# Two weight sums of the feed-forward tiles: adding DMAs in place of GpSimd additions

## The chip, the cores and the metric

The kernel runs on one core of one Trainium2 chip. The metric is the device time of one execution in microseconds; the number for the kernel before is the median of three runs. One further execution was profiled, and every view below comes from its trace.

## The reference, cut to what matters

The program computes two transformer blocks on a sequence of 512 tokens of width 1024, in 32-bit floats. Both end with a gated feed-forward network, and only these two networks are touched:

```
f = (silu(h @ w_gate) * (h @ w_up)) @ w_down          # first block
x = x + (silu(h @ w_ffn_gate) * (h @ w_ffn_up)) @ w_ffn_down   # second block
```

The hidden width is 2816, which is 22 tiles of 128 columns. Norms, attention and the other projections stand before, between and behind the two networks and are the same in both kernels.

## The kernel before, in words

**Arithmetic.** A 32-bit matrix is held as two parts, a high part (`hi`, a copy by ACT into the format that the matmul reads) and the rest (`lo`, a subtraction by DVE); a product takes three matmuls (hi·hi, hi·lo, lo·hi). So each weight tile that comes from HBM as `raw` is split by ACT and then DVE into `wt` or `u`.

**The products of one tile.** The feed-forward networks use a scheme of Strassen's kind. For tile f the gate and up products are formed from seven products of sums of weight blocks with sums of blocks of h. G is the gate's weight tile and U the up weight tile, each 128x1024 with a low half (columns 0 to 511) and a high half. `Tile.sums` (L390) forms four sums in place, in this order: G.lo += U.lo (L397), U.lo += U.hi (L398), U.hi = G.lo + U.hi (L399), G.hi = U.hi + G.hi (L400). All four run on GpSimd (POOL), 128x512 each. The third and fourth overwrite U.hi, so the split of the original U.hi (`w22`, DVE's u<-raw,u) has to be done before.

**Opening tiles ("head").** `first` and `second` are the two products with the unchanged gate weights. For the first 12 tiles of FFN 1 and the first 8 of FFN 2 (`t.head`) they are computed in an opening, before the main loop, from a load of the gate weights of their own; the other tiles do them in the main loop, and need the split of the unchanged G there.

**The main loop** (`ffn`, L414 on) runs over f from 0 to 21. An iteration does, among others: `finish(f-1)` on DVE, whose first operation t<-f,u reads PSUM; `left_g(f-1)`, whose lo halves are DVE's t<-t,t and u<-t,u with both inputs in SBUF; the products with s2 and s3; the splits of the next tile's U and G (`wb`, `wa`; DVE's wt<-raw,wt); the loads of tile f+3 and of a down weight; `blocks` of tile f+2 (the split of U.hi and, for a tile without an opening product, of G); the product with p1; `sums` of tile f+2; the down product of f-1; the products with a22 and p4. Between the products DVE reads PSUM banks (t<-u,tp, t<-f,t) that the next product goes on accumulating into.

**What sets the order.** `behind` fixes the order on PE, ACT and DVE in the main loop to the order of the code. POOL and the load queue (SP) are left to the scheduler. On POOL it puts the first two additions of the next tile behind the last two of this one, so in time they run as soon as that tile's loads have landed. All loads are issued by SP, 512 KB each; six raw buffers go round, three to an iteration, and a load waits until DVE and ACT have split what its buffer held.

Of the kernel before, what the change touches and what calls it, by code (L numbers as in the profile page):

```python
# [13 lines left out]
ALU = mybir.AluOpType  # L14
# [20 lines left out]
def transformer_pair(ctx: ExitStack, tc: tile.TileContext, A: dict, out: bass.AP, spill: dict):  # L35
# [6 lines left out]
    nc = tc.nc  # L42
# [340 lines left out]
    class Tile:  # L383
# [8 lines left out]
        def sums(self):  # L392

            lo, hi = slice(0, 512), slice(512, 1024)
            G, U = self.G, self.U
            add = nc.gpsimd.tensor_tensor
            add(G[:, lo], G[:, lo], U[:, lo], op=ALU.add)  # L397
            add(U[:, lo], U[:, lo], U[:, hi], op=ALU.add)  # L398
            add(U[:, hi], G[:, lo], U[:, hi], op=ALU.add)  # L399
            add(G[:, hi], U[:, hi], G[:, hi], op=ALU.add)  # L400

# [867 lines left out]
    U, Y, G = u_fill, pool_fill, gate_fill  # L1269
# [317 lines left out]
```

## Time and profile before

| | |
|---|---|
| Median of three runs | 1355.0 us (1354.44 to 1356.34) |
| Profiled execution, its own time | 1355.67 us |
| Its span, first to last instruction | 1354.0 us |
| Granted TensorE clock, mean | 0.992 of full speed |
| PE busy | 1298.9 us, 96% |
| DVE busy | 983.5 us, 73% |
| ACT busy | 733.4 us, 54% |
| POOL busy | 367.8 us, 27% |
| HBM read and written | 167.88 MB and 12.58 MB |

The busy times are unions of the engine's instructions over the span; a busy PE is not PE at its peak, since matmuls overlap and their ends are modelled. Idle time that a view puts down to a releaser (`<-DVE t L363`) is time in which the engine waited for that engine's instruction. Times in the timelines are microseconds from the span's start. The main loop of FFN 1 lies at about 275 to 530 us, that of FFN 2 at about 960 to 1230.

### The profile page before, as it was taken

How to read it: one execution, taken by the hardware profiler on the slowest of the kernel's cores; microseconds unless marked ns; L12 is line 12 of the kernel's file. 1: busy time of each engine (PE TensorE's matmuls, PEld its weight loads, DVE VectorE, ACT ScalarE, POOL GpSimd, SP SyncE). 2: the span in 40 equal slices, each digit the busy share in tenths (PEclk: the TensorE clock that was granted, in tenths of full speed). 3: DMA queues.
4: the chain of work that ended last, by engine and by line, in shares of the span. 5: the costliest groups of instructions: out<-in, count | busy, mean ns of one | idle time of the engine just before them, and what ended most of it. 6: DMA issues, size and time to landing. Idle time of an engine off the chain costs nothing.

```text
span 1354.0 us, 20845 instructions
## 1 busy us (share of the span) xinstructions
PE 1298.9 (96%) x7724; PEld 1109.6 (82%) x7724; DVE 983.5 (73%) x1840; ACT 733.4 (54%) x1332; POOL 367.8 (27%) x363
## 2 busy tenths in 40 slices
PE   8889999999999999999898999999999999999997
PEld 6656767988899998888676778879889999998886
DVE  5889677988888666866986662666788766767555
ACT  6578877644445443544776563525444554544453
POOL 1433232135543440000323011110354344320002
PEclk9999999999999999999999999999999999999999
DMA  7203123544443344832212335554344433437441
GB/s 280 89 32 127 62 82 121 172 131 151 144 152 124 111 140 153 282 125 89 75 63 70 125 127 187 193 203 141 125 141 141 140 110 125 138 108 255 140 138 62
DMA packets 56309, 181.81 MB, mean 134 GB/s; under 512 B 8592, under 2 KB 8976, under 8 KB 56208
## 3 DMA queue, kind: packets, MB, share of 16 engines
q1 hardware_dynamic: 56064, 180.49, 40.6%
q8 instruction: 60, 0.98, 0.3%
q14 instruction: 41, 0.34, 0.1%
q10 hardware_dynamic: 144, 0.00, 0.0%
HBM read 167.88 MB, written 12.58 MB: 133 GB/s over the span
## 4 chain that ended last, share of the span: by engine, by line
PE 54%; DVE 13%; issue 7%; ACT 3%; DMA 2%; POOL 1%; SPq 0%; DVEq 0%; POOLq 0%; ACTq 0%
PE f L349 14%; PE tp L349 10%; PE f L166 4%; PE f L168 4%; PE f L167 4%; DVE t L363 4%; PE acc L166 3%; PE acc L167 3%; PE acc L168 3%; DVE u L363 2%; DVE wt L363 1%; DVE p L1203 1%; DVE wt L161 1%; PE acc L349 1%; PE av L168 1%
## 5 line engine op out<-in xcount | busy, mean ns | idle before, releaser
L349 PE MATMUL tp<-sh,wt 128*128 128x256 f32 x1584 | 208.0, 286 | 5.3 <-DVE sh L57 3.6
L349 PEld LDWEIGHTS tp<-sh,wt 128*128 128x128 f32 x1584 | 200.4, 194 | 13.2 <-DVE t L363 6.8
L360 ACT ACTIVATE wt<-raw 128x1024 fp32r<-128x1024 f32 x152 | 155.6, 1051 | 85.6 <-issue 66.5
L363 DVE TENSOR_TENSOR wt<-raw,wt 128x1024 fp32r<-128x1024 f32 x152 | 190.0, 1250 | 2.0 <-ACT wt L360 1.7
L161 DVE TENSOR_TENSOR wt<-raw,wt 128x1024 fp32r<-128x1024 f32 (+1 forms) x88 | 108.8, 1240 | 49.3 <-ACT wt L160 48.4
L397 POOL TENSOR_TENSOR raw<-raw,raw 128x512 f32<-128x512 f32 x44 | 62.2, 1413 | 286.0 <-DVE wt L363 171.1
L166 PE MATMUL f<-wt,u 128*128 128x512 f32 x280 | 112.5, 403 | 4.6 <-ACT wt L254 2.4
L168 PE MATMUL f<-wt,u 128*128 128x512 f32 x280 | 112.4, 401 | 1.0 <-DVE u L255 1.0
L160 ACT ACTIVATE wt<-raw 128x1024 fp32r<-128x1024 f32 (+1 forms) x88 | 91.4, 1046 | 39.6 <-PE f L168 11.6
L167 PE MATMUL f<-wt,u 128*128 128x512 f32 x280 | 111.5, 399 | 0.6 <-DVE wt L161 0.6
L166 PE MATMUL f<-u,wt 128*128 128x512 f32 x272 | 107.5, 395 | 0.3 <-ACT nx L1104 0.2
L167 PE MATMUL f<-u,wt 128*128 128x512 f32 x272 | 107.0, 393 | 0.0
L168 PE MATMUL f<-u,wt 128*128 128x512 f32 x272 | 106.8, 393 | 0.0
L349 PE MATMUL f<-u,wt 128*128 128x256 f32 x744 | 99.4, 283 | 0.0
L349 PEld LDWEIGHTS f<-u,wt 128*128 128x128 f32 x744 | 93.5, 192 | 0.0
L363 DVE TENSOR_TENSOR u<-tp,u 128x256 f32<-128x256 f32 x88 | 36.6, 416 | 72.9 <-PE tp L349 72.8
L399 POOL TENSOR_TENSOR raw<-raw,raw 128x512 f32<-128x512 f32 x44 | 57.1, 1297 | 85.3 <-DVE u L363 76.9
L349 PE MATMUL f<-sh,u 128*128 128x256 f32 x528 | 71.9, 286 | 5.0 <-DVE t L363 5.0
L349 PEld LDWEIGHTS f<-sh,u 128*128 128x128 f32 x528 | 66.2, 191 | 7.8 <-DVE t L363 7.8
L349 PE MATMUL f<-sh,wt 128*128 128x256 f32 x528 | 70.9, 284 | 0.0
L360 ACT ACTIVATE u<-u 128x256 f32<-128x256 f32 x44 | 18.4, 417 | 96.4 <-DVE u L363 96.4
L254 ACT ACTIVATE wt<-raw 128x1024 fp32r<-128x1024 f32 x44 | 45.5, 1058 | 44.1 <-PE acc L168 24.5
(336 smaller groups left out, 3027.2 us busy)
## 6 DMA issues: line engine op xcount, KB each, us to landing
raw<-in_w_down SPq DMA_DIRECT2D x44, 512.0 KB, 3.9
raw<-in_w_ffn_down SPq DMA_DIRECT2D x44, 512.0 KB, 3.9
raw<-in_w_gate SPq DMA_DIRECT2D x34, 512.0 KB, 4.3
raw<-in_w_ffn_gate SPq DMA_DIRECT2D x30, 512.0 KB, 4.3
raw<-in_w_out SPq DMA_DIRECT2D x24, 512.0 KB, 3.7
raw<-in_w_up SPq DMA_DIRECT2D x22, 512.0 KB, 3.8
raw<-in_w_ffn_up SPq DMA_DIRECT2D x22, 512.0 KB, 3.7
raw<-in_w_in SPq DMA_DIRECT2D x11, 512.0 KB, 5.0
```

What stands on the lines that cost most here:

```text
L160: sca.activation(w[:, 0, c], raw[:, c], AF.Copy)
L161: pl["lo"].tensor_tensor(w[:, 1, c], raw[:, c], w[:, 0, c].bitcast(F32), op=ALU.subtract)
L166: nc.tensor.matmul(ps, lhsT=st[0], rhs=mv[0], start=first, stop=False)
L167: nc.tensor.matmul(ps, lhsT=st[0], rhs=mv[1], start=False, stop=False)
L168: nc.tensor.matmul(ps, lhsT=st[1], rhs=mv[0], start=False, stop=last)
L254: sca.activation(hi, src, AF.Copy)
L349: i = nc.tensor.matmul(ps[:, :256], lhsT=st[a], rhs=mv[b], start=first and k == 0 and n == 0, stop=k == 3 and n == 2, skip_group_check=True)
L360: return behind("act", nc.scalar.activation(out, src, fn))
L363: return behind("dve", nc.vector.tensor_tensor(out, a, b, op=op))
L397: add(G[:, lo], G[:, lo], U[:, lo], op=ALU.add)
L399: add(U[:, hi], G[:, lo], U[:, hi], op=ALU.add)
L1203: vec.tensor_tensor_scan(c[:, n - 1::-1], ones.to_broadcast([P, n]) if nq == 1 else restart[:, :n], e[:, n - 1::-1], 0.0, op0=ALU.mult, op ...
```

## The change

For tiles f > 1 that had their first products in the opening (`head`), the first two sums are no longer GpSimd additions. POOL issues two DMAs that add: the up weights are read from HBM a second time, the low half added into G.lo and the high half into U.lo, 256 KB each. That makes 10 tiles in FFN 1 and 6 in FFN 2, so 32 DMAs in place of 32 additions. The third and fourth sum, tiles 0 and 1, and the tiles without an opening product stay as they were.

```diff
             add = nc.gpsimd.tensor_tensor
-            add(G[:, lo], G[:, lo], U[:, lo], op=ALU.add)
-            add(U[:, lo], U[:, lo], U[:, hi], op=ALU.add)
+            if self.f > 1 and self.head:
+                nc.gpsimd.dma_start(out=G[:, lo], in_=self.wu[self.f][:, lo], accum_op=ALU.add)
+                nc.gpsimd.dma_start(out=U[:, lo], in_=self.wu[self.f][:, hi], accum_op=ALU.add)
+            else:
+                add(G[:, lo], G[:, lo], U[:, lo], op=ALU.add)
+                add(U[:, lo], U[:, lo], U[:, hi], op=ALU.add)
             add(U[:, hi], G[:, lo], U[:, hi], op=ALU.add)
             add(G[:, hi], U[:, hi], G[:, hi], op=ALU.add)
```

In the changed kernel the DMAs are lines 398 and 399, the additions that stay for other tiles 401 and 402, and the third and fourth sum lines 403 and 404. The order of instructions on PE, DVE, ACT and SP is the same in both; on POOL it is not. The adding DMAs are waited for by the third sum, by ACT's and DVE's splits of the sums, and by the next load into the same buffer.

POOL's order in the steady part of FFN 1, before: raw_818 and raw_819 are G and U of tile 6, raw_831 and raw_832 G and U of tile 7.

```order
L397 TENSOR_TENSOR raw_818_3718<-raw_818_3718,raw_819_3720 128x512
L398 TENSOR_TENSOR raw_819_3720<-raw_819_3720 128x512
L399 TENSOR_TENSOR raw_819_3720<-raw_818_3718,raw_819_3720 128x512
L400 TENSOR_TENSOR raw_818_3718<-raw_819_3720,raw_818_3718 128x512
L397 TENSOR_TENSOR raw_831_3830<-raw_831_3830,raw_832_3832 128x512
L398 TENSOR_TENSOR raw_832_3832<-raw_832_3832 128x512
L399 TENSOR_TENSOR raw_832_3832<-raw_831_3830,raw_832_3832 128x512
L400 TENSOR_TENSOR raw_831_3830<-raw_832_3832,raw_831_3830 128x512
```

The same place on POOL in the changed kernel:

```order
L398 DMA raw_818_3718<-in_w_up 128x512
L399 DMA raw_819_3720<-in_w_up 128x512
L399 DMA raw_832_3832<-in_w_up 128x512
L403 TENSOR_TENSOR raw_819_3720<-raw_818_3718,raw_819_3720 128x512
L404 TENSOR_TENSOR raw_818_3718<-raw_819_3720,raw_818_3718 128x512
L398 DMA raw_831_3830<-in_w_up 128x512
L403 TENSOR_TENSOR raw_832_3832<-raw_831_3830,raw_832_3832 128x512
L404 TENSOR_TENSOR raw_831_3830<-raw_832_3832,raw_831_3830 128x512
```

The DMA into U of the odd tile 7 now stands ahead of the third sum of the even tile 6, and the two DMAs of a tile are issued apart; so it goes for the pairs 4 and 5 to 10 and 11, and in FFN 2 for 4 and 5, 6 and 7.

POOL's order at the first tiles of FFN 1, before: raw_761 and raw_762 are G and U of tile 1, raw_764 and raw_765 of tile 2, raw_777 and raw_778 of tile 3.

```order
L397 TENSOR_TENSOR raw_764_3346<-raw_764_3346,raw_765_3348 128x512
L398 TENSOR_TENSOR raw_765_3348<-raw_765_3348 128x512
L399 TENSOR_TENSOR raw_762_3337<-raw_761_3335,raw_762_3337 128x512
L400 TENSOR_TENSOR raw_761_3335<-raw_762_3337,raw_761_3335 128x512
L399 TENSOR_TENSOR raw_765_3348<-raw_764_3346,raw_765_3348 128x512
L400 TENSOR_TENSOR raw_764_3346<-raw_765_3348,raw_764_3346 128x512
L397 TENSOR_TENSOR raw_777_3392<-raw_777_3392,raw_778_3394 128x512
L398 TENSOR_TENSOR raw_778_3394<-raw_778_3394 128x512
```

And in the changed kernel:

```order
L398 DMA raw_764_3346<-in_w_up 128x512
L399 DMA raw_765_3348<-in_w_up 128x512
L403 TENSOR_TENSOR raw_762_3337<-raw_761_3335,raw_762_3337 128x512
L404 TENSOR_TENSOR raw_761_3335<-raw_762_3337,raw_761_3335 128x512
L398 DMA raw_777_3392<-in_w_up 128x512
L403 TENSOR_TENSOR raw_765_3348<-raw_764_3346,raw_765_3348 128x512
L404 TENSOR_TENSOR raw_764_3346<-raw_765_3348,raw_764_3346 128x512
L399 DMA raw_778_3394<-in_w_up 128x512
```

Here the DMA into G of tile 3 has moved ahead of the third sum of tile 2.

## Rows read from the trace of the kernel before

**Rows 1.** The page: busy us, share of the span, instructions of each engine.
```profile
PE 1298.9 (96%) x7724; PEld 1109.6 (82%) x7724; DVE 983.5 (73%) x1840; ACT 733.4 (54%) x1332; POOL 367.8 (27%) x363
```
**Rows 2.** Timeline of DVE, FFN 1: start, us, operation, count [idle before <-releaser].
```profile
317.76 0.42 DVE L363 TENSOR_TENSOR t<-f,u 128x256 f32<-128x256 f32 x1 [1.46 <-PE f L349]
...
320.11 1.52 DVE L363 TENSOR_TENSOR t<-t,t 128x256 fp32r<-128x256 f32 x1
321.56 1.52 DVE L363 TENSOR_TENSOR u<-t,u 128x256 fp32r<-128x256 f32 x1
...
326.53 0.41 DVE L363 TENSOR_TENSOR t<-f,t 128x256 f32<-128x256 f32 x1
```
**Rows 3.** Timeline of DVE, FFN 1, the iteration at 383.64 and the next one's start.
```profile
383.64 0.42 DVE L363 TENSOR_TENSOR t<-f,u 128x256 f32<-128x256 f32 x1 [1.47 <-PE f L349]
384.10 0.84 DVE L363 TENSOR_TENSOR t<-u,t 128x256 f32<-128x256 f32 x2
...
385.99 0.41 DVE L363 TENSOR_TENSOR t<-t,t 128x256 fp32r<-128x256 f32 x1
386.33 0.41 DVE L363 TENSOR_TENSOR u<-t,u 128x256 fp32r<-128x256 f32 x1
...
389.60 0.68 DVE L363 TENSOR_TENSOR u<-raw,u 128x512 fp32r<-128x512 f32 x1
...
391.33 0.41 DVE L363 TENSOR_TENSOR t<-f,t 128x256 f32<-128x256 f32 x1
...
393.58 0.42 DVE L363 TENSOR_TENSOR t<-f,u 128x256 f32<-128x256 f32 x1 [1.01 <-PE f L349]
```
**Rows 4.** Timeline of POOL, FFN 1: tile 6's first additions, tile 7's, tile 12's.
```profile
319.77 1.58 POOL L397 TENSOR_TENSOR raw<-raw,raw 128x512 f32<-128x512 f32 x1 [1.33 <-DMA raw<-in_w_up]
321.43 1.37 POOL L398 TENSOR_TENSOR raw<-raw 128x512 f32<-128x512 f32 x1
...
330.79 1.55 POOL L397 TENSOR_TENSOR raw<-raw,raw 128x512 f32<-128x512 f32 x1 [1.37 <-DMA raw<-in_w_gate]
...
391.49 1.29 POOL L397 TENSOR_TENSOR raw<-raw,raw 128x512 f32<-128x512 f32 x1 [7.17 <-DVE wt L363]
```
**Rows 5.** Groups of DVE, 298 to 376 us: count | busy us, mean ns | idle before.
```profile
L363 DVE TENSOR_TENSOR wt<-raw,wt 128x1024 fp32r<-128x1024 f32 x22 | 26.6, 1210 | 0.0
L363 DVE TENSOR_TENSOR t<-t,t 128x256 fp32r<-128x256 f32 x8 | 12.2, 1521 | 0.0
```
**Rows 6.** Timeline of PE: the products with a22 and p4 in both iterations.
```profile
324.93 1.69 PE L349 MATMUL tp<-sh,wt 128*128 128x256 f32 x12
327.00 1.70 PE L349 MATMUL f<-sh,u 128*128 128x256 f32 x12 [0.38 <-DVE t L363]
...
390.50 1.60 PE L349 MATMUL tp<-sh,wt 128*128 128x256 f32 x12
391.94 1.60 PE L349 MATMUL f<-sh,u 128*128 128x256 f32 x12
```
**Rows 7.** Timeline of DVE: starts of iteration 1 (FFN 1), 1 and 6 (FFN 2).
```profile
284.88 0.42 DVE L363 TENSOR_TENSOR t<-f,u 128x256 f32<-128x256 f32 x1 [1.04 <-PE f L349]
...
969.81 0.42 DVE L363 TENSOR_TENSOR t<-f,u 128x256 f32<-128x256 f32 x1 [1.01 <-PE f L349]
...
1024.46 0.42 DVE L363 TENSOR_TENSOR t<-f,u 128x256 f32<-128x256 f32 x1 [1.46 <-PE f L349]
```
**Rows 8.** SP's issue of a load; raw loads' landing, 290 to 345; issues by tensor.
```profile
320.25 0.33 SPq L273 DMA_DIRECT2D raw<-in_w_up  x1
...
DMA to landing us min/median/max: 3.4/3.7/4.7
...
row<-in_norm_ffn_pre SPq DMA_DIRECT2D x1, 512.0 KB, 9.1
raw<-in_w_pool SPq DMA_DIRECT2D x1, 256.0 KB, 2.6
```
**Rows 9.** FFN 1, 298 to 375: busy us of each engine, PE clock, DMA share, GB/s.
```profile
298.00:375.00 77.00, 73.34 (x508) 66.07 (x507) 66.53 (x92) 31.71 (x50) 38.78 (x29) 1.00 0.47 144
```

## The prediction

> **What bounds the kernel now.** I read first the page's busy times: TensorE (PE) is busy 96% of the span, VectorE (DVE) 73%, GpSimd (POOL) 27% [rows 1]. So POOL's work counts only through what it does to PE. The change lies in the two feed-forward loops (FFN 1 with 12 opening tiles, FFN 2 with 8), so the second view is the timeline of DVE and of POOL in one iteration of FFN 1. I count from the start of DVE's first operation of an iteration, t<-f,u, as "+". In the iteration that starts at 317.76 the two operations t<-t,t and u<-t,u, 128x256 with both inputs in SBUF, take 1.52 us each [rows 2]. The same two take 0.41 us in the iteration at 383.64 [rows 3]. What differs is POOL: at 319.77 it begins the first two additions of a tile (lines 397 and 398, just as the tile's load lands), and they cover exactly these two operations [rows 4]; in the iteration at 383.64 POOL begins no addition before 391.49 [rows 4]. Eight of eight t<-t,t between 298 and 376 us average 1521 ns [rows 5]. DVE is held for 2 x 1.11 = 2.2 us, and runs without a pause from 317.76 to 326.94.
>
> Does PE feel it? Two matmul groups wait for DVE to have read a PSUM bank. In the held iteration the group tp<-sh,wt begins at 324.93 and f<-sh,u at 327.00, after an idle 0.38 us put down to DVE; in the free one the same groups begin at 390.50 and 391.94 without any [rows 6]. Counted from the iteration's start that is +7.17 and +9.24 against +6.86 and +8.30. So PE loses 0.3 us at the first place and 0.6 more at the second, and another 0.1 in the matmuls behind each restart. The free iteration lasts 393.58 - 383.64 = 9.94 us [rows 3]; a held one 1.04 more, as the next paragraph shows.
>
> **The change part by part.**
>
> 1) Removed: 32 POOL additions of 128x512 (two for each of the tiles 2 to 11 of FFN 1 and 2 to 7 of FFN 2), about 1.37 to 1.58 us each where they meet DVE [rows 4], some 46 us of POOL. None of that lies on the path itself; what does is DVE's hold. The adds of tile f+2 run in iteration f. For FFN 1 the iterations 1 to 9 reach from 284.88 to 383.64 [rows 7, 3]: 98.76 us (10.97 each), where nine free ones take 9 x 9.94 = 89.46, so 9.30 us can be won. For FFN 2 the iterations 1 to 5 reach from 969.81 to 1024.46 [rows 7]: 54.65 against 5 x 9.94 = 49.70, so 4.95 us. Together **14.25 us**. Tile 2's pair runs before the loops, where I count nothing, with 1 us either way as the bound (the price of one held iteration).
>
> Is 9.94 a fair floor? The free iteration has the same five products and one down step on PE, and DVE has even one split of 1.21 us more in it than an opening iteration has (it prepares the first tile without an opening product). Its t<-f,t ends at 391.74 = +8.10, and PE needs it at +8.30 [rows 3, 6]. Without the extra split it would end near +6.9. So DVE can lose some 1.3 us in an opening iteration before PE sees anything.
>
> 2) Added: 32 DMAs of 256 KB that POOL issues. No row of before shows such a DMA, so both its prices are bounded. The issue on POOL: at least the 0.33 us that SP's queue takes for one [rows 8]; above, 2.6 us, twice an addition. I take 1.3, as long as the addition that it replaces [rows 4]. From issue to landing: at least the 2.6 us of a plain 256 KB load; at most the 9.1 us of the slowest load of the trace. I take 3.7, the median of the 512 KB loads in this loop, since the add moves 256 KB in and must read as much of its target [rows 8].
>
> 3) Added waits: the third addition (line 399, now 403) waits for both adding DMAs, besides DVE's u<-raw,u as before. Behind it stand on POOL the fourth addition and the next tile's DMA issue; ACT's splits of both weight tiles wait for these, and PE uses them one iteration later. By the free iteration u<-raw,u ends at 389.60 + 0.68, +6.64; so 403 runs from about +6.7 and 404 ends near +9.4, before the iteration's end, while DVE reads from PSUM. The next operation of DVE with two SBUF inputs, t<-u,t, comes 0.46 into the next iteration (384.10 in the free one), at +10.4. Up to there 403 and 404 hold nobody, and 1.3 us beyond it are covered by DVE's slack. Hence 403 may start as late as +9.0 without a price.
>
> Odd tiles: the gate load of tile 7 lands at 330.79 [rows 4], and its iteration begins 10.97 after 317.76, so +2.06 now. It is issued when DVE ends a split that will come 2.2 us earlier in an iteration that is 1.04 shorter, so +0.9. Issue 1.3, landing 3.7: +5.9, before +6.64. Covered; even at 8 us for both it would be +8.9. Even tiles: the last of their loads lands at 319.77, +2.0 now [rows 4], and +0.9 then: the same sum. But POOL's order puts the issue of the next (odd) tile's up add ahead of the even tile's 403, and that load is issued at 320.25, +2.49, behind a split that was not held; with 3.7 it lands at +6.2 [rows 8]. With the issue of 1.3 us, 403 starts at +7.5 and 404 ends at +10.2. Covered by a hair, and by 1.5 us with DVE's slack.
>
> 4) Traffic: the loop moves 144 GB/s at a DMA share of 0.47 [rows 9], some 1.58 MB an iteration. With 0.52 MB more in 9.94 us the share goes to 0.47 x 2.10/1.58 x 10.98/9.94 = 0.69, to 0.86 if an added byte costs double. Under 1, so the loads stay hidden, though later: that belongs to the rivals. The Trainium skill, page "DMA: Bandwidth & Descriptors", section "Issuing engines are not separate DMA queues", says that DMAs run on the same 16 DMA engines and interleave whoever issues them. This speaks against the change: a second queue brings no bandwidth; no run here shows it yet, and by it alone the chance of the first rival below rises.
>
> Sum, against the profiled execution: span 1354.0, its own time 1355.67, the median of the runs 1355.0. 1355.67 - 14.25 = 1341.4; from the median 1340.8. I forecast **1341**.
>
> **The rivals.**
> - Even tiles slide. If the load and the issue together need over 6.5 us (4.7, the slowest load in the loop [rows 8], with 1.8 do it), 403 of the even tiles starts after +9.0 and 404 runs into the next iteration's t<-u,t and splits, which then are held as today. Six tiles are even (four in FFN 1, two in FFN 2): 6 x 1.04 = 6.2 us come back, **1347.6**. For it: the share of 0.69. Against: the median load takes 3.7, and then the issue may take 2.8.
> - No gain. The DMA issue itself holds DVE as an addition does, or every tile slides by over 2 us: the hold only moves, **1355**. For it: the first issues would fall at +0.9 to +2.2, beside DVE operations with two SBUF inputs. Against: an issue reads no weights from SBUF. The Trainium skill's page "SBUF — State Buffer", section "Who interferes with whom", says that a DVE operation with two SBUF inputs contends with a GpSimd instruction that reads SBUF, not with one that only writes it; by this the issue would hold nothing and the sum stays. The trace agrees on the first half (1.52 against 0.41 us); no row shows the second.
> - Slower: the adds land so late that PE starves. In the next iteration t<-f,t has to end by +8.30; ahead of it on DVE stand u<-raw,u (0.68) and the split of the tile that 404 forms (1.21 [rows 5]), ahead of that ACT's half of the split (taken as long). So 404 must end by +4.8 there, and 403, two additions earlier, may start at 4.8 - 2.7 + 9.94 = +12.1 at the latest. With the load at +0.9 that allows 11.2 us from issue to landing; at 12.2 the iteration is as long as today's, and from there each further us costs up to 14 us. At 13.2: **1369**. It decides from 12.2 us; the slowest load of the trace took 9.1 [rows 8].
>
> **How the numbers follow.** Full gain, 1341: 0.58. Even tiles slide, 1348: 0.18. No gain: 0.10. Slower: 0.09. Better than 1338, because tile 2 or the loads gain as well: 0.05. The low end is 1338, the full gain with some 3 us for what I counted at zero (tile 2 in both loops, 2 x 1.04, and rounding); the high end is 1353, which holds the second case and a part of the third and leaves out the rest and the slower one, about 0.19 with the low tail. About 0.2% (2.7 us) is what a measurement of this kernel tells from no change: faster 0.79, within it 0.10, slower 0.11.
>
> **What would show it.** Right: t<-t,t and u<-t,u at 0.41 us in iterations 1 to 9 and 1 to 5; t<-f,u every 9.94 us; no idle of PE put down to DVE at f<-sh,u. Step 2 is read from POOL's issue and from issue to landing of the adds, step 3 from the starts of 403: +6.7 for odd, +7.5 for even tiles. Wrong: 403 waiting for a DMA beyond +9.0, DVE's t<-u,t or wt<-raw at 1.5 us and more behind it, or PE waiting for ACT's splits.

## The result, and the profile after

The changed kernel takes **1345.0 us** (median of six runs, 1342.4 to 1346.4) against 1355.25 for the kernel before beside it: ratio 0.9921, 95% interval 0.9907 to 0.9935. A second measurement, in the last group of experiments, gave 1345.9 and 0.9925 (0.9907 to 0.9943). It is faster by 0.8%, inside the stated range, 4 us above the 1341 that was forecast.

The page of the profiled execution, the row that answers to [rows 1]:

```profile
span 1343.3 us, 20899 instructions
PE 1293.4 (96%) x7724; PEld 1109.8 (83%) x7724; DVE 966.6 (72%) x1840; ACT 733.9 (55%) x1332; POOL 348.0 (26%) x363
...
q0 software_dynamic: 4608, 8.39, 4.0%
```

The new queue q0 carries the 32 adding DMAs, 8.39 MB. DVE is busy 17 us less with the same 1840 instructions: these are the holds that went, less those that came back at another place (without these sums, in the run "Nothing in their place" below, DVE is busy 953.5 us, 30 less than before). The groups of DVE in FFN 1 from 289 to 374 us (count | busy us, mean ns) answer to [rows 5]:

```profile
L363 DVE TENSOR_TENSOR t<-u,t 128x256 f32<-128x256 f32 x16 | 11.4, 751 | 0.3
...
L363 DVE TENSOR_TENSOR t<-t,t 128x256 fp32r<-128x256 f32 x8 | 3.3, 415 | 0.0
L363 DVE TENSOR_TENSOR u<-t,u 128x256 fp32r<-128x256 f32 x8 | 3.3, 414 | 0.0
```

t<-t,t fell from 1521 to 415 ns, as forecast. But t<-u,t, the second thing that an iteration does on DVE, averages 751 ns where a free one takes about 0.4: in a few iterations the hold has come back at another place. Ten of the fourteen opening iterations last 9.93 to 9.94 us. Four do not: in FFN 1 iteration 3 (10.61) and 5 (10.54), in FFN 2 iteration 3 (11.40) and 5 (10.97). The loops' ends, to be set against [rows 3, 7] (DVE, first operation of iterations 1 and 10 of FFN 1, 1 and 6 of FFN 2):

```profile
283.06 0.42 DVE L363 TENSOR_TENSOR t<-f,u 128x256 f32<-128x256 f32 x1 [1.07 <-PE f L349]
...
373.77 0.42 DVE L363 TENSOR_TENSOR t<-f,u 128x256 f32<-128x256 f32 x1 [1.02 <-PE f L349]
...
961.33 0.42 DVE L363 TENSOR_TENSOR t<-f,u 128x256 f32<-128x256 f32 x1 [1.07 <-PE f L349]
...
1013.51 0.42 DVE L363 TENSOR_TENSOR t<-f,u 128x256 f32<-128x256 f32 x1 [1.46 <-PE f L349]
```

FFN 1: 98.76 us became 90.71, a gain of 8.05 of the 9.30 that could be won. FFN 2: 54.65 became 52.18, 2.47 of 4.95. Together 10.5 us of the span's 10.7. What is missing to 14.25 is 3.7 us, and it lies in those four iterations.

**Where it went.** POOL around iterations 2 and 3 of FFN 1, which begin at 292.99 and 302.93 (start, us, operation [idle before <-releaser]), set against [rows 4]:

```profile
293.91 0.87 POOL L398 DMA_DIRECT2D raw<-in_w_up  x1 [0.31 <-issue]
294.61 1.06 POOL L399 DMA_DIRECT2D raw<-in_w_up  x1
302.16 0.86 POOL L399 DMA_DIRECT2D raw<-in_w_up  x1 [6.49 <-DVE u L363]
302.72 1.61 POOL L403 TENSOR_TENSOR raw<-raw,raw 128x512 f32<-128x512 f32 x1
304.41 1.37 POOL L404 TENSOR_TENSOR raw<-raw,raw 128x512 f32<-128x512 f32 x1
```

DVE in the same place:

```profile
295.27 0.41 DVE L363 TENSOR_TENSOR t<-t,t 128x256 fp32r<-128x256 f32 x1
295.61 0.41 DVE L363 TENSOR_TENSOR u<-t,u 128x256 fp32r<-128x256 f32 x1
...
298.88 0.68 DVE L363 TENSOR_TENSOR u<-raw,u 128x512 fp32r<-128x512 f32 x1
...
302.93 0.42 DVE L363 TENSOR_TENSOR t<-f,u 128x256 f32<-128x256 f32 x1 [1.01 <-PE f L349]
303.39 2.67 DVE L363 TENSOR_TENSOR t<-u,t 128x256 f32<-128x256 f32 x2
```

Tile 4's third sum (403) could have run at 299.6, when u<-raw,u ended: of its tile's two DMAs it reads only the one into G, and that had landed at 297.6 (293.91 + 3.7). It started at 302.72, +9.73, because POOL's queue holds the odd tile 5's up add (302.16) ahead of it, and that add waited for tile 5's load, which landed at 301.5. (The view names DVE as the releaser of that add. But 403 starts 1.2 us behind the load's landing here as at tile 9 below, where the view names the load.) So the third and fourth sums ran into the next iteration, over t<-u,t, and PE had 0.20 us of idle again at f<-sh,u of iteration 3, 311.79 - 302.93 = 8.86 us behind its start:

```profile
311.79 1.70 PE L349 MATMUL f<-sh,u 128*128 128x256 f32 x12 [0.20 <-DVE t L363]
```

How late the odd load was: first that one load (issued at 295.4), then all loads of 285 to 374 us (min, median, max; [rows 8] has 3.4, 3.7, 4.7 for before):

```profile
DMA to landing us min/median/max: 6.1/6.1/6.1
...
DMA to landing us min/median/max: 3.7/4.6/6.1
```

Tile 9's load, issued at 336.44, landed after 4.5 us; there 403 of tile 8 ran at +8.13 and iteration 7 took 9.94. So the same queue order is harmless or costs 0.6 to 1.5 us, depending on how long that one load takes. Why it took 6.1 us at tile 5 and 4.5 at tile 9 no row shows.

### The profile page after: what moved, and what is told of

It reads as the page before. It is cut to its first block, busy times and chain, and to the rows that moved or that the text cites. A ratio compares the mean times of both kernels' runs of the same rounds, so it can differ in the third digit from the quotient of the medians.

```text
span 1343.3 us, 20899 instructions
## 1 busy us (share of the span) xinstructions
PE 1293.4 (96%) x7724; PEld 1109.8 (83%) x7724; DVE 966.6 (72%) x1840; ACT 733.9 (55%) x1332; POOL 348.0 (26%) x363
## 3 DMA queue, kind: packets, MB, share of 16 engines
q0 software_dynamic: 4608, 8.39, 4.0%
## 4 chain that ended last, share of the span: by engine, by line
PE 61%; DVE 8%; issue 6%; ACT 3%; DMA 1%; POOL 1%; DVEq 0%; POOLq 0%; ACTq 0%
PE f L349 15%; PE tp L349 13%; PE f L168 5%; PE f L167 5%; PE f L166 4%; PE acc L167 4%; PE acc L166 4%; PE acc L168 4%; DVE t L363 1%; DVE wt L161 1%; DVE p L1207 1%; PE av L166 1%; PE av L167 1%; PE av L168 1%; DMA raw<-in_w_out 1%
## 5 line engine op out<-in xcount | busy, mean ns | idle before, releaser
L349 PE MATMUL tp<-sh,wt 128*128 128x256 f32 x1584 | 204.2, 283 | 3.6 <-DVE sh L57 3.6
L363 DVE TENSOR_TENSOR wt<-raw,wt 128x1024 fp32r<-128x1024 f32 x152 | 189.0, 1244 | 2.2 <-ACT wt L360 2.1
L401 POOL TENSOR_TENSOR raw<-raw,raw 128x512 f32<-128x512 f32 x28 | 36.8, 1316 | 267.5 <-DVE wt L363 171.5
L403 POOL TENSOR_TENSOR raw<-raw,raw 128x512 f32<-128x512 f32 x44 | 59.8, 1358 | 44.9 <-DVE u L363 39.1
L255 DVE TENSOR_TENSOR wt<-raw,wt 128x1024 fp32r<-128x1024 f32 x44 | 53.4, 1223 | 21.4 <-ACT wt L254 21.3
```

Of the source, the lines that this page charges most:

```text
L255: (lo_eng or vec).tensor_tensor(lo, src, hi.bitcast(F32), op=ALU.subtract)
L349: i = nc.tensor.matmul(ps[:, :256], lhsT=st[a], rhs=mv[b], start=first and k == 0 and n == 0, stop=k == 3 and n == 2, skip_group_check=True)
L363: return behind("dve", nc.vector.tensor_tensor(out, a, b, op=op))
```

## The experiments

The theory at this point: a POOL addition holds a DVE operation with two SBUF inputs; DVE can lose about 1.2 us an iteration unseen; what remains comes from even tiles' third sums that wait behind an odd tile's add, whose load is slow in the crowd. The rivals: the DMAs cost something of their own; POOL's order alone does it; or any POOL instruction holds DVE.

**Order on POOL.** POOL is held to the order of the code, so each tile's two DMAs stand directly ahead of its own third sum.

```diff
-            add = nc.gpsimd.tensor_tensor
+            def add(*a, **kw):
+                behind("pool", nc.gpsimd.tensor_tensor(*a, **kw))
...
-                nc.gpsimd.dma_start(out=G[:, lo], ...)
+                behind("pool", nc.gpsimd.dma_start(out=G[:, lo], ...))
...
-                nc.gpsimd.dma_start(out=U[:, lo], ...)
+                behind("pool", nc.gpsimd.dma_start(out=U[:, lo], ...))
```

> The changed kernel with POOL held to the order of the code: both adding DMAs of a tile, then its third and fourth sum, then the next tile's DMAs; so no odd tile's DMA stands ahead of an even tile's third sum. Theory (the even tiles were late because of that place in POOL's queue): the four long iterations of the changed kernel (10.61 and 10.54 us in FFN 1, 11.40 and 10.97 in FFN 2, together 3.8 us over 9.94) shrink to 9.94, the time is 1345.0 - 3.8 = 1341.2 us, and the third sums of even tiles start at about +8.4, when their own DMA has landed. Rival (the adding DMAs crowd the loads, whatever the order): the third sums still start near +9.7, the long iterations stay, 1345 us.

Measured: 1342.2 us, ratio 0.9907 (0.9889 to 0.9924). In FFN 2 all five iterations take 9.94; in FFN 1 eight of nine do (one 10.13). But iteration 10, outside the fourteen and 9.94 in both kernels, takes 11.48, since tile 11's third sum came at +9.82 of iteration 9 and held t<-u,t of iteration 10 for 1.65 us. That iteration already has one split more ([rows 3]: t<-f,t ends at +8.10, and the prediction has PE need it at +8.30), so nearly all of it, 1.54, is lost:

```profile
367.58 0.88 POOL L399 DMA_DIRECT2D raw<-in_w_up  x1 [2.43 <-DMA raw<-in_w_gate]
368.17 1.19 POOL L400 DMA_DIRECT2D raw<-in_w_up  x1
374.35 2.72 POOL L397 TENSOR_TENSOR raw<-raw,raw 128x512 f32<-128x512 f32 x2 [4.99 <-DMA raw<-in_w_up]
```

(POOL; DMA lines are 399 and 400 here, all additions 397.) Issued together beside three loads, tile 11's adds took 6.6 and 8.7 us to land. The third sum started as soon as the first had landed (367.58 + 6.6), 2.5 us before the second: it waits for the add into G alone, not for both, as the section on the change and the prediction's step 3 have it. So the even tiles' third sums did not start at the expected +8.4 either, but four of the six at +6.65 and two at +8.1. The order accounts for most of the four long iterations; the crowd then shows at another place. Neither theory nor rival alone.

**Nothing in their place.** The floor:

```diff
-            if self.f > 1 and self.head:
-                nc.gpsimd.dma_start(...)
-                nc.gpsimd.dma_start(...)
-            else:
+            if not (self.f > 1 and self.head):
```

> Leaves out the first two sums of the 16 tiles altogether: neither additions nor adding DMAs (the weights of those tiles are then not the sums). It is the floor of the change. Theory: all 14 iterations at 9.94 us and 1341 us, so the DMAs themselves cost what the changed kernel is longer, about 4 us. Rival (the DMAs cost elsewhere too, by the loads of the opening or the end): 1339 us or less.

Measured: 1340.6 us, 0.989 (0.9864 to 0.9917); all fourteen iterations 9.94, and 403's counterpart starts at +6.64 in every one, the value that was read from the free iteration. So the gain to be had is, as near as the interval tells, the 14 us of the loops, and the changed kernel lies 4 us over this floor.

**One DMA in place of two.** The first sum stays an addition:

```diff
+            add(G[:, lo], G[:, lo], U[:, lo], op=ALU.add)
             if self.f > 1 and self.head:
-                nc.gpsimd.dma_start(out=G[:, lo], in_=self.wu[self.f][:, lo], accum_op=ALU.add)
                 nc.gpsimd.dma_start(out=U[:, lo], in_=self.wu[self.f][:, hi], accum_op=ALU.add)
             else:
-                add(G[:, lo], G[:, lo], U[:, lo], op=ALU.add)
                 add(U[:, lo], U[:, lo], U[:, hi], op=ALU.add)
```

> Only the second of the two sums (into the up tile) is a DMA; the first is an addition on POOL as before, for all tiles. Theory (an addition holds one DVE operation by 1.1 us, and DVE can lose some 1.3 us in such an iteration before PE sees it): t<-t,t at 1.5 us, u<-t,u at 0.41, all 14 iterations at 9.94 to 10.0, and with half the added traffic and no odd DMA ahead of an even tile's third sum 1341 to 1342 us. Rival (the hold of one operation costs PE half of what two cost): 0.5 us in each of 13 iterations, 1348 us.

Measured: **1340.7 us**, 0.9893 (0.9875 to 0.9910), better than the changed kernel and as short as the floor; all fourteen iterations 9.94. POOL and DVE in one of them:

```profile
304.40 1.43 POOL L397 TENSOR_TENSOR raw<-raw,raw 128x512 f32<-128x512 f32 x1 [1.61 <-DMA raw<-in_w_gate]
306.13 0.87 POOL L399 DMA_DIRECT2D raw<-in_w_up  x1 [0.30 <-POOL raw L397]
310.08 1.28 POOL L402 TENSOR_TENSOR raw<-raw,raw 128x512 f32<-128x512 f32 x1 [3.08 <-DVE u L363]
...
304.59 1.53 DVE L363 TENSOR_TENSOR t<-t,t 128x256 fp32r<-128x256 f32 x1
306.04 0.41 DVE L363 TENSOR_TENSOR u<-t,u 128x256 fp32r<-128x256 f32 x1
...
DMA to landing us min/median/max: 3.8/4.4/4.7
```

(The last line is for the nine adding DMAs of FFN 1 from 282 to 372 us.) The addition still holds t<-t,t for 1.1 us, and PE does not notice. The third sum waits for DVE alone and starts at +7.76 in thirteen of the fourteen iterations (once at +7.43). It does not read what this DMA writes: the one of 306.13 lands 4.4 us later, at about 310.5, when the third sum has already begun, and so it is in eleven of the fourteen. The sum that was moved is thus the one with time to spare, since only the splits of the next iteration need it. The order is clean too: the DMA must wait until the addition has read U, so no odd tile's DMA comes early.

**A longer hold.** The kernel above with one more, shorter addition behind the first, which adds U's first 256 columns once more:

```diff
             if self.f > 1 and self.head:
+                add(G[:, 0:256], G[:, 0:256], U[:, 0:256], op=ALU.add)
```

> The kernel with the second sum as a DMA in the 16 tiles, with one more addition of 128x256 on POOL behind the first (it adds a part of the up tile to the gate tile once more, so the sums are wrong). Theory (DVE can lose about 1.2 us in an opening iteration; one hold is 1.1, two cost 1.04 of 2.2): the holds come to some 1.8 us, the iterations to 10.5 to 10.6, 14 of them 8 to 9 us over 1340.7, so 1349 us. Rival (there is no such threshold, one DVE operation is simply free): 9.94 and 1341, or 10.98 and 1355.

One run: 1348.4 us; ten of the fourteen iterations at 10.34 to 10.37 (10.5 to 10.6 were expected).

```profile
309.60 1.52 DVE L363 TENSOR_TENSOR t<-t,t 128x256 fp32r<-128x256 f32 x1
311.04 0.96 DVE L363 TENSOR_TENSOR u<-t,u 128x256 fp32r<-128x256 f32 x1
```

The holds are 1.11 + 0.55 = 1.66 us and cost 0.42; two whole holds, 2.22, cost 1.04 in the kernel before; one, 1.11, costs nothing. All three say that DVE can lose about 1.2 us in such an iteration. The other four iterations fit: where the additions met DVE for 1.31 to 1.33 us only, they took 10.02 or 10.03, and where they met it for 2.26 us, 10.93. There is a threshold, and it is close to where the prediction's 1.3 put it. That the time is so near to the expected 1349 is in part luck: the loops are 5.4 us over 9.94, and another 4.5 us lie ahead of them. Iteration 1 of FFN 1 begins at 286.93, in the kernel above at 282.44; the granted clock of 255 to 284 us was 0.88 here and 1.00 there.

**Fills that only write.** Four fills in place of the two sums:

```diff
-                nc.gpsimd.dma_start(...)
-                nc.gpsimd.dma_start(...)
+                for t in (G, G, U, U):
+                    nc.gpsimd.memset(t[:, lo], 0.0)
```

> Leaves out the first two sums of the 16 tiles and puts four GpSimd fills of 128x512 (two into each of the two targets) in their place, which write SBUF and read none (the weights are then not the sums). Theory (only POOL's reading holds a DVE operation with two SBUF inputs): t<-t,t and u<-t,u stay at 0.41 us beside the fills, iterations 9.94, about 1341 us. Rival (any POOL instruction on SBUF holds DVE): these operations at up to 0.5 us longer each, 0.9 us where a fill lies over them.

One run: 1339.9 us, all fourteen iterations 9.93 to 9.95. POOL and DVE (without a neighbour t<-u,t takes 0.42 us and the weight split 1.21; the fills mostly fall beside these, not beside t<-t,t):

```profile
323.59 1.11 POOL L399 MEMSET raw<- 128x512 f32 x2 [0.63 <-DMA raw<-in_w_gate]
...
323.40 0.76 DVE L363 TENSOR_TENSOR t<-u,t 128x256 f32<-128x256 f32 x2
324.08 1.22 DVE L363 TENSOR_TENSOR wt<-raw,wt 128x1024 fp32r<-128x1024 f32 x1
```

A POOL instruction that writes SBUF and reads none holds nothing: 50 operations of DVE with two SBUF inputs lay beside fills and no addition, all at their free durations. This is the half of the rule in the Trainium skill's page "SBUF — State Buffer", section "Who interferes with whom", that no row had shown before.

**The other one of the two.** The first sum is the DMA, the second the addition:

```diff
-                nc.gpsimd.dma_start(out=U[:, lo], ...)
-            else:
-                add(G[:, lo], ...)
-                add(U[:, lo], U[:, lo], U[:, hi], op=ALU.add)
+            else:
+                add(G[:, lo], ...)
+            add(U[:, lo], U[:, lo], U[:, hi], op=ALU.add)
```

> Only the first of the two sums (into the gate tile) is a DMA; the second is an addition on POOL. Its scheduled order puts the odd tile's addition ahead of the even tile's third sum, as the changed kernel does with the odd tile's DMA, at half the added traffic. Theory (an order like this costs only when the odd tile's load is late, and with half the traffic it lands in some 4.5 us): third sums of even tiles at about +8, iterations 9.94 to 10.2, 1341 to 1343 us. Rival (the order alone, at any traffic, makes the even tiles late): three or more of the six even tiles' following iterations at 10.5 or more, 1344 us and above.

Measured: 1346.1 us, 0.9931 (0.9915 to 0.9946); five iterations at 10.8 to 10.9. By the number the rival was right, but by neither mechanism: the third sums start at +8.9 at the latest and hold nothing. POOL and DVE in a long iteration, which begins at 295.47:

```profile
296.78 2.19 POOL L401 TENSOR_TENSOR raw<-raw 128x512 f32<-128x512 f32 x1
302.28 1.40 POOL L401 TENSOR_TENSOR raw<-raw 128x512 f32<-128x512 f32 x1 [3.30 <-DMA raw<-in_w_up]
...
302.45 1.77 DVE L363 TENSOR_TENSOR u<-raw,u 128x512 fp32r<-128x512 f32 x1
```

In four of the five, with the odd tile's addition moved up, one iteration holds two additions and the next none. The second hold falls on u<-raw,u (1.77 instead of 0.68); 2.2 us are lost together, and 0.95 is seen. In the fifth (FFN 2, iteration 1) the tail of the tile before and one addition hold t<-u,t for 2.1 us together. Held evenly, one an iteration, they would have cost nothing, as the run with one DMA shows.

**Half the bytes, same order.** Both DMAs cut to 256 columns (the other half of the sums is left out):

```diff
-                ...out=G[:, lo], in_=self.wu[self.f][:, lo]...
+                ...out=G[:, 0:256], in_=self.wu[self.f][:, 0:256]...
...
-                ...out=U[:, lo], in_=self.wu[self.f][:, hi]...
+                ...out=U[:, 0:256], in_=self.wu[self.f][:, 512:768]...
```

> The changed kernel with both adding DMAs cut to the first half of their columns (128x256 each; the other half of the two sums is left out): the same DMAs, waits and order on POOL, half the added bytes. Theory (the even tiles are late because loads and adds crowd each other on the DMA engines, and POOL's order hands an odd tile's late load on to the even tile's third sum): odd tiles' loads land in about 4.5 us, third sums of even tiles start before +9, no or one long iteration, 1340 to 1342 us. Rival (POOL's order alone, at any traffic): four long iterations, 1345 us.

Measured: 1340.0 us, 0.9892 (0.9876 to 0.9909): thirteen iterations 9.94, one (FFN 2, iteration 3) 10.67. POOL's order is that of the changed kernel, so the order alone does not make the even tiles late; the bytes are needed too. Over all loads of the loop nothing got quicker (median 4.9 us, up to 6.6), but these are not the ones that count. The odd tiles' six up loads for which POOL's queue waits landed after 5.3, 5.3, 3.9 and 4.4 us in FFN 1 and 6.2 and 5.2 in FFN 2; in the changed kernel the same six took 6.1, 6.1, 4.5, 4.9, 7.0 and 6.5. The slowest, 6.2, belongs to the long iteration: the even tile's 403 began at +9.78 there, and at +8.9 or earlier in the other five.

**All tiles.** The kernel with one DMA, with the second sum by DMA in the later tiles as well:

```diff
-            if self.f > 1 and self.head:
+            if self.f > 1:
```

> The second sum as a DMA for all tiles from 2 on, those without an opening product too; the first an addition. In the later iterations (12.82 us in every kernel so far) PE waits for nobody although POOL's additions hold DVE there. Theory (what DVE loses there is no one's loss): iterations stay at 12.82 and the time is that of the kernel with this DMA in the 16 tiles alone, 1340.7 us within 2. Rival (those iterations are held as well): 12.6 or less each, 1337 us or less.

Measured: 1339.05 us, 0.9879 (0.9865 to 0.9894), the shortest of the variants that compute the whole result; not to be told from the 16 tiles alone, and beside it the changed kernel took 1345.9. The later iterations stay at 12.82 (starts 407.67 and 420.49): DVE is held less there and nobody gains.

**The changed kernel again.**

> The changed kernel once more, beside the variants on the same chip. By its first measurement 1345 us, 0.992 of before; which of the even tiles' following iterations are long (two of four in FFN 1, both in FFN 2 in its first trace) should vary if the late landings are a matter of how loads and adds meet on the DMA engines, and stay if the order alone decides.

1345.9 us. Long this time are iterations 5, 7 and 9 of FFN 1 (10.39, 11.41, 11.03) and 3 and 5 of FFN 2 (11.62, 11.19): always those that follow an even tile's sums, but others in FFN 1 than before. POOL and DVE at iterations 6 and 7, the latter from 345.35:

```profile
345.39 0.86 POOL L399 DMA_DIRECT2D raw<-in_w_up  x1 [6.83 <-ACT u L360]
345.95 1.62 POOL L403 TENSOR_TENSOR raw<-raw,raw 128x512 f32<-128x512 f32 x1
...
345.81 3.48 DVE L363 TENSOR_TENSOR t<-u,t 128x256 f32<-128x256 f32 x2
```

The price follows one line. Counted from the start of its own iteration, the even tile's 403 began at +9.52, 10.16, 10.31, 10.54 and 10.75 in this trace, and the next iteration was longer than 9.94 by 0.45, 1.09, 1.25, 1.47 and 1.68; in the first trace +9.66, 9.73, 10.09 and 10.52 went with 0.60, 0.67, 1.03 and 1.46. Each time the loss is the start less 9.06, and none where 403 started by +9.0. DVE's rows say the same more directly. For each iteration, add up by how much DVE's operations outlast their free durations: that hold, less 1.22 to 1.27 us, is the loss in all 30 long opening iterations of these two traces and of the runs with the order, the longer hold, the other one of the two and half the bytes (1.17 to 1.26 in the kernel before, where two whole holds, 2.22, cost 1.04).

## Why the prediction was right, and where it was off

The sign, the mechanism and the floor were right. Step 1 (9.94 us for an iteration without a hold, 14.25 us to be won) is what every kernel without late sums shows; the fourteen iterations of four kernels are at 9.93 to 9.95. The slack of 1.3 us is about 1.25. The latest harmless start of 403, +9.0, is +9.06. That holds for a 403 right behind a DMA issue, which is 0.34 us longer than one by itself (1.62 against 1.28); without such an issue a start at +9.60 in the order run cost 0.19, so there it is +9.4.

The step that was mis-sized is the load of the odd tile in step 3: "with 3.7 it lands at +6.2". It was the median of a loop that moved 144 GB/s at a share of 0.47. In the changed kernel the median is 4.6, and the four odd loads that mattered took 6.1, 6.1, 7.0 and 6.5 us. The issue estimate held: 403 starts 1.1 to 1.2 us after that load has landed, against the 1.3 assumed. So load and issue together took 7.2 to 8.1 us there, over the 6.5 from which the first rival was said to decide, and 5.7 at tile 9, where nothing happened. The forecast and this rival were thus both half true: four of the six even tiles slid. Its price, 1.04 us for each, was off as well. It took the hold of today as a cap; the loss grows with the lateness, 0.60 to 1.46. Four such tiles cost 3.7 us, which is the distance from 1341 to 1345.

Step 3 also has the third sum wait for both adding DMAs, where it waits for the one into G alone; this did not make the even tiles late, POOL's queue did. And the starts of 403 that were named as the sign of being right, +6.7 for odd and +7.5 for even tiles, did not come: the even ones lie at +8.1 to +10.5, and the odd ones at +7.2 to +9.4, since they wait for u<-raw,u, which comes later when the late sums of the tile before hold DVE. Only the floor kernel shows +6.64 throughout.

Traffic, step 4, was bounded at 0.69 to 0.86 and came to 0.79 (289 to 374 us; the last three columns are PE clock, DMA share and GB/s), first the changed kernel, then one DMA of two, then none:

```profile
289.00:374.00 85.00, 84.59 (x609) 79.71 (x608) 66.25 (x110) 37.07 (x58) 37.01 (x34) 1.00 0.79 213
...
289.00:374.00 85.00, 85.00 (x623) 81.00 (x622) 70.75 (x112) 37.62 (x60) 44.44 (x34) 1.00 0.64 188
...
289.00:374.00 85.00, 85.00 (x617) 80.75 (x616) 61.10 (x110) 36.51 (x57) 23.24 (x18) 1.00 0.49 162
```

The conclusion drawn there, "under 1, so the loads stay hidden", was the weak point: a share of 0.79 hides the mean, not the one load for which POOL's queue waits. The sentence of the Trainium skill's page "DMA: Bandwidth & Descriptors", section "Issuing engines are not separate DMA queues", on the 16 DMA engines that all issuing engines share spoke for this rival, and the loads' 3.7 to 4.6 us agree with it.

The rival "no gain" fell: the issue on POOL holds nothing. The one at 294.61 lasts until 295.67, and t<-t,t at 295.27 takes 0.41 beside it; so do the 17 operations of its size with two SBUF inputs that met an issue and no addition, 0.41 to 0.43 us each. The slower rival needed 12.2 us from issue to landing; the adds took 4.1 in the median and 7.6 at most. What counted at zero, tile 2 before the loops, is not shown by the 0.2 us between the span's 10.7 and the loops' 10.5, in which two larger differences nearly cancel. Iteration 1 of FFN 1 began 1.82 us earlier (283.06 for 284.88), and the stretch between the loops was 1.39 us longer (373.77 to 961.33, for 383.64 to 969.81). Both go with TensorE's clock: the granted clock of 255 to 284 us was 0.88 of full speed before (7 of the 29 us at half speed, 1.2 GHz for 2.4) and 1.00 in this trace of the changed kernel, and that of 600 to 800 us 1.00 before and 0.98 here. Its second trace has 0.88 at 255 to 284 us too, and its iteration 1 begins at 285.26; beside 284.88 that leaves 0.4 us for tile 2, inside the bound of 1.

## What to carry to other kernels

An engine far from being the bound can still set the pace by holding another one: look for one instruction form with two durations, and for what runs beside the long ones. Then measure how much the held engine can lose unseen, and remove no more than that; here one DMA of two, into the sum that the next addition does not read, brought the whole gain at half the traffic, and two brought less. And when a DMA is put on a queue whose order a scheduler sets, look at what waits behind it: its price is that of the slowest load it can meet, not of the median.

## What the runs showed of the hardware that was not expected

An added byte costs the DMA engines about twice a loaded one: the loop's loads, 162 GB/s, take a share of 0.49, so 0.30 for each 100 GB/s; one add per tile brings 26 GB/s and 0.15, two bring 51 GB/s and 0.30, so 0.58 for each 100. An adding DMA of 256 KB lands in 4.1 us at the median, longer than the 3.7 of the loop's 512 KB loads in the kernel before, where the DMA engines were less busy. And the issue costs POOL about 0.9 us, though its slice (0.85 to 1.06 us) overlaps that of the next instruction: 403 starts 0.56 us after the issue ahead of it began, but then lasts 1.62 us instead of 1.28, and 404 starts 2.25 us after that issue (302.16 to 304.41), where it starts 1.36 us after the start of a 403 by itself.
